# A hybrid encoder layer on one core: first norm from token-major x, first two tiles side by side, tables in the weights' buffers, residual stored from ScalarE, another end

## The chip, the cores and the metric

The kernel runs on 1 core of one Trainium2 chip. The metric is the device time of one execution in microseconds (us). A profile comes from one profiled execution, and its times count from the start of that execution's span. The engines are named as in the profile: PE is TensorE, DVE is VectorE, ACT is ScalarE, POOL is GpSimd, SP is SyncE, which only issues transfers (DMAs).

## What is computed

One layer on 512 tokens of width 2048, in float32:

```python
xn = rms_norm(x, attn_norm_g)                       # over D_MODEL = 2048
proj = xn @ w_in                                    # 2048 -> 5120
u_val, u_gate, q, k, v = split(proj)                # 1024 columns each
# group A: GLU -> depthwise conv, width 31 -> LayerNorm -> silu
y_conv = silu(layer_norm(conv31(u_val * sigmoid(u_gate))))
# group B: 2-D neighbourhood attention, 16 heads of 64, on an 8 x 64 grid,
# window 8 x 16, learned bias rpb per head
y_na = softmax(q k^T / 8 + bias) v
x = x + concat(rms_norm(y_conv), rms_norm(y_na)) @ w_out
up = conv3(rms_norm(x, ffn_norm_g) @ w_up)          # 2048 -> 2 x 5632
gate, val = split(up)
x = x + (silu(gate) * val) @ w_down                 # 5632 -> 2048
return rms_norm(x, final_norm_g)
```

## The kernel before

Activations lie with channels on the 128 partitions and the 512 tokens in the free dimension. Every float32 product is made from two parts: an operand is split into `hi`, rounded to the format of the fast matmul by ScalarE (L115 for weights, L256 for x), and `lo`, the remainder, by VectorE (L116, L257). `mm3` then issues three matmuls (hi by hi, L128; hi by lo, L131; lo by hi, L132) of 512 columns.

Weights come in units of 128 x 1024 (512 KB), one SP load each into the ring `raw` (tag "raw", NR = 9 buffers of 4 KB a partition, L92 to L117), and are split into `whi` and `wlo` (NW = 4 buffers each). A list `plan` holds the making of each unit in the order of use, and `weights()` makes them AHEAD = 3 units before they are used. All other activations of 2 KB a partition share one pool of NT = 75 tiles, `t2`. A scheduler puts the instructions of each engine in order, by priority (the place in the program, moved by `shifted`), by readiness and by free buffers; instructions under `pin` keep their order. Each engine, and each engine's own queue of DMA issues, then runs in the order written.

The stages, in order of time:

- **Head** (L248 to L287). SP loads the parameters `prm` (all per-channel factors, 336 KB), then 16 tiles of x (256 KB each) and, among them, the four units of the first two tiles of the projection, gate and value. Each x tile is multiplied by the norm's factor g1 and split. The norm's root is applied to the products later, by `rstd`.
- **Norm** (`stats1`, `rsqrt_steps`). The squares of the 16 tiles are summed on VectorE (L202), summed over partitions by matmuls with `ones` (L216), and the root is spread over the partitions by a matmul of `ones` with a diagonal `dg` (L229, L232).
- **Projections** (`project`, `glu`, `qkv`), 40 tiles of 128 output channels in the order of `ORDER`, each with a PSUM buffer of the three of tag "mm". After each half of a tile `tick` moves side work on by one step: the norm, the heads' attention, group A's LayerNorm. `gated` evacuates a gate and value pair and does the convolution of width 31 on VectorE; its results `y` lie in four buffers of the ring `raw` until group A ends. `sum_ahead` forms sums of the down weights in DRAM with GpSimd's DMAs.
- **Attention** (`attend`), one pair of heads at a time. `table` loads the bias (two DMAs of 256 KB into `t2` tiles for each half), `scores` (L414) fills the one PSUM tile `sc`, VectorE adds the bias (L421), then softmax; `turn` transposes into PSUM (L441) and copies to `pt` (L445); `values` multiplies with v.
- **Output projection** (`out_half`), twice 16 tiles. In the second, `after` adds the residual, and `turned` transposes it to tokens on partitions and stores it from SP to DRAM, four 64 KB pieces a tile (L559).
- **Up product** (`up`, `hidden`), 44 tiles, by a 2 x 2 scheme with seven products instead of eight (L656, L659). The hidden tiles go to DRAM, but for the last KEEP = 4; `again` loads them back during the last tile.
- **Down product** (`product2`, L777 to L779), the same scheme, seven products; `operand` makes the activations' split of each (L738, L739) as a part of the plan.
- **End** (`taken`, `ready`, `write`). The last product's last four steps of the sum over hidden channels are done one output block at a time; `ready` adds the residual (L829), squares (L831) and multiplies by the final norm's factor (L832), `write` forms the root (L839 to L846), scales (L851, L853) and stores, from SP and from GpSimd (L855).

## Time and profile before

| | |
|---|---|
| median of 3 runs | 2020.2 us (2019.28 to 2020.69) |
| the profiled execution: its time | 2021.06 us |
| its span | 2019.1 us |
| mean granted TensorE clock | 0.996 |
| first matmul starts | 8.04 us |
| busy: PE, DVE, ACT, POOL | 99%, 80%, 55%, 11% |
| DMA, mean | 221 GB/s |

A row of the timeline has the start, the duration, the engine and line, the operation, output <- input, how many, and in brackets the idle time before it and what ended it. A row of the waits has who waited for whom, us in total, times, and the longest. Rows of windows have the stretch, its length, then the busy time and count of PE, weight loads, DVE, ACT and POOL, the granted clock, the DMA engines' busy share and GB/s. SPq and POOLq stand for an engine's queue of DMA issues.

### The profile page before, as it was taken

To read this page: it belongs to the slowest core of one execution; us is meant where nothing else is said; L and a number is where in the kernel's file an instruction comes from. 1 tells how busy PE (TensorE), PEld (TensorE's weight loads), DVE (VectorE), ACT (ScalarE), POOL (GpSimd) and SP (SyncE) were. 2 spreads that over 40 slices of the span, in tenths; PEclk is the share of its full clock that TensorE was granted. 3 is DMA by queue.
4 is the path that set the end of the run, shared out by engine and by line. 5 is a ranking of instruction groups with operands and counts; after the bars stand their busy time and mean duration, and the time that the engine had idled before them with its cause. 6 is when DMAs were issued, how large, how long until landed. Compare 5 with 4: busy or idle time off the path is not lost.

```text
span 2019.1 us, 28450 instructions
## 1 busy us (share of the span) xinstructions
PE 1990.3 (99%) x10511; PEld 1682.7 (83%) x10511; DVE 1608.5 (80%) x2311; ACT 1104.1 (55%) x1724; POOL 230.2 (11%) x318
## 2 busy tenths in 40 slices
PE   8999999998999999999999999999999999999997
PEld 6888888877788888888888888888888888888886
DVE  7985798497556888888888888888888898886764
ACT  6244424446535666666666666666666654554663
POOL 0111111111001111111111111111110400000000
PEclk9999999999999999999999999999999999999999
DMA  7677677676758879899999898998986976665562
GB/s 257 167 222 182 171 176 207 175 191 196 232 140 214 209 204 253 248 247 256 249 255 258 245 267 233 264 242 256 259 236 192 344 261 217 213 217 192 194 212 101
DMA packets 141755, 446.81 MB, mean 221 GB/s; under 512 B 15920, under 2 KB 24112, under 8 KB 140208
## 3 DMA queue, kind: packets, MB, share of 16 engines
q1 hardware_dynamic: 98352, 293.99, 42.6%
q0 software_dynamic: 43264, 151.01, 34.4%
q8 instruction: 82, 1.34, 0.3%
q14 instruction: 57, 0.47, 0.1%
HBM read 426.07 MB, written 111.15 MB: 266 GB/s over the span
## 4 chain that ended last, share of the span: by engine, by line
PE 97%; ACT 1%; DMA 1%; DVE 1%; issue 0%; SPq 0%; POOLq 0%; POOL 0%; DVEq 0%
PE pu L656 25%; PE pu L659 12%; PE pj L128 7%; PE pj L132 7%; PE pd L778 7%; PE pd L779 7%; PE pd L777 7%; PE pj L131 7%; PE po L128 3%; PE po L131 3%; PE po L132 3%; PE pu L128 2%; PE pu L131 2%; PE pu L132 2%; PE po L454 1%; PE sc L414 1%
## 5 line engine op out<-in xcount | busy, mean ns | idle before, releaser
L115 ACT ACTIVATE whi<-raw 128x1024 fp32r<-128x1024 f32 x574 | 607.2, 1059 | 719.2 <-PE pj L131 220.6
L116 DVE TENSOR_TENSOR wlo<-raw,whi 128x1024 fp32r<-128x1024 f32 x574 | 701.1, 1222 | 295.5 <-ACT whi L115 268.2
L656 PE MATMUL pu<-xc,whi 128*128 128x512 f32 x2112 | 748.8, 399 | 0.0
L659 PE MATMUL pu<-xc,wlo 128*128 128x256 f32 x2112 | 593.2, 281 | 0.0
L656 PEld LDWEIGHTS pu<-xc,whi 128*128 128x128 f32 x2112 | 397.0, 188 | 97.0 <-issue 0.2
L659 PEld LDWEIGHTS pu<-xc,wlo 128*128 128x128 f32 x2112 | 399.1, 189 | 0.3 <-issue 0.2
L128 PE MATMUL pj<-xh,whi 128*128 128x512 f32 x640 | 254.4, 399 | 8.0 <-ACT whi L115 8.0
L131 PE MATMUL pj<-xl,whi 128*128 128x512 f32 x640 | 251.4, 393 | 0.0
L132 PE MATMUL pj<-xh,wlo 128*128 128x512 f32 x640 | 251.2, 393 | 0.0
L777 PE MATMUL pd<-whi,ho 128*128 128x512 f32 x616 | 239.5, 389 | 1.6 <-ACT ho L738 1.6
L779 PE MATMUL pd<-whi,ho 128*128 128x512 f32 x616 | 239.6, 389 | 0.6 <-DVE ho L739 0.6
L778 PE MATMUL pd<-wlo,ho 128*128 128x512 f32 x616 | 239.8, 389 | 0.0
L328 DVE SCALAR_TENSOR_TENSOR y<-ch,prm,y 128x507 f32<-128x507 f32 (+14 forms) x240 | 169.8, 739 | 3.3
L128 PEld LDWEIGHTS pj<-xh,whi 128*128 128x128 f32 x640 | 121.3, 189 | 36.3 <-ACT whi L115 9.4
L132 PEld LDWEIGHTS pj<-xh,wlo 128*128 128x128 f32 x640 | 120.9, 189 | 27.9 <-DVE wlo L116 1.5
L131 PEld LDWEIGHTS pj<-xl,whi 128*128 128x128 f32 x640 | 121.2, 189 | 24.7 <-issue 0.7
L184 POOL DMA_DIRECT2D ws<-in_w_down x88 | 79.4, 903 | 545.4 <-DMA ws<-ws 273.6
L777 PEld LDWEIGHTS pd<-whi,ho 128*128 128x128 f32 x616 | 115.7, 188 | 26.3 <-ACT ho L738 1.9
L779 PEld LDWEIGHTS pd<-whi,ho 128*128 128x128 f32 x616 | 115.7, 188 | 25.0 <-DVE ho L739 1.2
L778 PEld LDWEIGHTS pd<-wlo,ho 128*128 128x128 f32 x616 | 115.7, 188 | 24.1 <-DVE wlo L116 0.3
L605 POOL DMA_DIRECT2D raw<-in_w_up x88 | 85.3, 969 | 368.0 <-DMA raw<-in_w_up 142.2
L128 PE MATMUL pu<-xc,whi 128*128 128x256 f32 x352 | 99.7, 283 | 0.5 <-ACT xc L546 0.5
(170 smaller groups left out, 2500.4 us busy)
## 6 DMA issues: line engine op xcount, KB each, us to landing
raw<-in_w_up SPq DMA_DIRECT2D x220, 512.0 KB, 7.3
ws<-in_w_down POOLq DMA_DIRECT2D x132, 512.0 KB, 7.4
raw<-in_w_up POOLq DMA_DIRECT2D x88, 512.0 KB, 9.4
raw<-ws SPq DMA_DIRECT2D x88, 512.0 KB, 3.4
raw<-in_w_in SPq DMA_DIRECT2D x80, 512.0 KB, 5.0
raw<-in_w_down SPq DMA_DIRECT2D x66, 512.0 KB, 3.7
ws<-ws POOLq DMA_DIRECT2D x44, 512.0 KB, 7.2
raw<-in_w_out SPq DMA_DIRECT2D x32, 512.0 KB, 5.2
```

What stands on the lines that cost most here:

```text
L115: i = nc.scalar.activation(hi[:, :n], raw[:, :n], AF.Copy)
L116: j = nc.vector.tensor_sub(lo[:, :n], raw[:, :n], hi[:, :n].bitcast(F32))
L128: i = nc.tensor.matmul(ps, hi[:, a], mh, start=start, stop=False, skip_group_check=more)
L131: nc.tensor.matmul(ps, hi[:, a], ml, start=False, stop=False, skip_group_check=more)
L132: return nc.tensor.matmul(ps, lo[:, a], mh, start=False, stop=stop, skip_group_check=more)
L328: nc.vector.scalar_tensor_tensor(y[:, a:b], h[:, a + j - PAD:b + j - PAD], prm[:, o + j:o + j + 1], y[:, a:b], op0=ALU.mult, op1=ALU.add)
L605: nc.gpsimd.dma_start(a[c], w_up[f, q2], accum_op=ALU.add)
L656: i = nc.tensor.matmul(ps, hi[:, w], m, start=k == 0 and not more, stop=False, skip_group_check=more)
L659: i = nc.tensor.matmul(ps[:, :H], lo[:, w], m[:, :H], start=False, stop=k == U - 1, skip_group_check=more)
L777: nc.tensor.matmul(ps[i], h[:, t], wh[:, d], start=start and not more, stop=False, skip_group_check=more)
L778: nc.tensor.matmul(ps[i], h[:, t], wl[:, d], start=False, stop=False, skip_group_check=more)
L779: return nc.tensor.matmul(ps[i], h[:, tl], wh[:, d], start=False, stop=stop, skip_group_check=more)
```

## The change

Five things are changed together.

- **Head.** ScalarE does a one-element copy behind the memset of `ones`, and TensorE 11 matmuls of 128 x 128 on `ones` into an unused PSUM tile. The norm's factor `g1` is loaded by itself from ScalarE's queue, the rest of `prm` after x. The gate and the value tile run side by side (`first_glu`): at each tile of x six matmuls, three for each. The first half of their weights is loaded in pieces of 2, 2 and 4 tiles of 128 columns.
- **First norm.** `stats1` loads x a second time, with tokens on partitions (`xn`, eight loads of 512 KB into the ring `raw`), squares on ScalarE with the sum along the free dimension, and forms the root from there (`root_steps`).
- **Tables.** The two tables of a half come in one load of 512 KB into one buffer of the ring `raw`. The copy of the transposed softmax to `pt` gets an earlier priority.
- **Residual and hidden tiles.** The residual is one DRAM tensor, stored with one DMA a tile from ScalarE's queue. `again` loads six hidden tiles at a time instead of eight, and the down product's first operand is made during the second product of the last up tile.
- **End.** `ready` in the last product comes at an earlier priority; for one block of each pair the factor g is applied in `write` together with the scale. The root is taken from the sum directly, with scale and bias on ScalarE, and one product is fused. Stores go out from SP and ScalarE.

```diff
+WARM = 11
+SOONER = 100
...
-    nc.sync.dma_start(prm, par)
+    g1 = consts.tile([P, KD], F32, name="g1")
+    nc.scalar.dma_start(g1, par[:, :KD])
...
     nc.vector.memset(ones, 1.0)
+    idle = t2("idle")
+    nc.scalar.activation(idle[:, :1], ones[:, :1], AF.Copy)
+    ps = psm.tile([P, S], F32, tag="mm", name="warm")
+    for _ in range(WARM):
+        nc.tensor.matmul(ps[:, :P], ones, ones, start=True, stop=True)
...
+    def split_x(k):
         x1.append(t2("x"))
-        last = pin(nc.sync.dma_start(x1[k], xT[k]))
+        i = pin(nc.sync.dma_start(x1[k], xT[k]))
...
+    def piece(n, k0, k1):
+        m = (k1 - k0) * P
+        raw, hi, lo = t2("we")[:, :m], t2("weh", F32R)[:, :m], t2("wel", F32R)[:, :m]
+        pin(nc.sync.dma_start(raw, w_in[n, :, k0 * P:k1 * P]))
+        pin(nc.scalar.activation(hi, raw, AF.Copy))
+        pin(nc.vector.tensor_sub(lo, raw, hi.bitcast(F32)))
+        return [(hi, lo, k - k0) for k in range(k0, k1)]
...
+    for ks, ws in (((0,), (0, 2)), ((1,), (2, 4)), ((2, 3), (4, 8)), (range(4, 8), ())):
+        for k in ks:
+            split_x(k)
+        for j, n in enumerate((NC_, 0)):
+            if ws:
+                early[j] += piece(n, *ws)
+    for j, n in enumerate((NC_, 0)):
+        raw, i = raw_unit(w_in[n, :, U * P:2 * U * P], U * P)
...
+    for k in range(U, KD):
+        last = split_x(k)
+    last = pin(nc.sync.dma_start(prm, par))
...
     def stats1():
-        for k in range(KD):
-            sum_sq(acc1, x1[k], k == 0)
-        for _ in range(3):
-            yield
-        rstd.append((yield from rsqrt_steps(acc1, D, "rstd1")))
+        part = sm.tile([P, S // P, 2], F32, tag="ss", name="ss")
+        for t in range(S // P):
+            for i in range(2):
+                x = t4([P, D // 2], "xn")
+                nc.sync.dma_start(x, xn[t * P:(t + 1) * P, i * D // 2:(i + 1) * D // 2])
+                nc.scalar.activation(x, x, AF.Square, accum_out=part[:, t, i:i + 1])
+            if t < S // P - 1:
+                yield
+        sums = sm.tile([P, S // P], F32, tag="s1", name="s1")
+        nc.vector.tensor_reduce(sums, part, axis=AX.X, op=ALU.add)
+        rstd.append((yield from root_steps(sums, D, "rstd1")))
...
+    def first_glu():
+        two = [psm.tile([P, S], F32, tag="mm", name="pj") for _ in range(2)]
+        for u in range(KD // U):
+            ws = weights(), weights()
+            for k in range(U):
+                kk = u * U + k
+                for ps, w in zip(two, ws):
+                    hi, lo, at = w[k]
+                    m = mm3(ps, (hi, lo), at, xs[kk][0], xs[kk][1], kk == 0, kk == KD - 1)
+            for _ in range(2):
+                tick(m)
+        late.append(lambda: gated(0, *two))
...
-                nc.scalar.activation(pt, ps, AF.Copy)
+                with shifted(-SOONER):
+                    nc.scalar.activation(pt, ps, AF.Copy)
...
         def table(b0):
-            for j in range(2):
-                tb = t2("tab").rearrange("p (i k) -> p i k", i=2)
-                i = nc.sync.dma_start(tb, tab[2 * p + j][:, b0 // 2:b0 // 2 + 2])
-                if p == 0:
-                    pin(i)
-                tabs.append(tb)
+            tb = t4([P, 2, 2, 2 * P], "tab")
+            i = nc.sync.dma_start(tb, tab[2 * p:2 * p + 2, :, b0 // 2:b0 // 2 + 2].rearrange("h p k c -> p h k c"))
+            if p == 0:
+                pin(i)
+            tabs.append(tb)
...
-        o = d % (S // P) * P
-        for t in range(S // P):
-            nc.sync.dma_start(xt[t][d * P // S][:, o:o + P], r[:, t, :])
+        nc.scalar.dma_start(xt[:, :, d * P:(d + 1) * P].rearrange("t p k -> p t k"), r)
...
-            plan.append(lambda c=c, k=k: (unit2(c, k), operand(c, k)))
+            plan.append(lambda c=c, k=k: (unit2(c, k), pre.pop(0) if pre else operand(c, k)))
...
+    pre = []
+
     def again(at, i):
-        for _ in range(8):
+        if at == 1:
+            pre.extend(operand(TURN2[0], k) for k in order2[:KEEP // 2 - 1])
+        for _ in range(6):
...
-            nc.vector.tensor_mul(x[i], x[i], gs[d])
+            if i not in fused:
+                nc.vector.tensor_mul(x[i], x[i], gs[d])
             yield
...
         nc.vector.tensor_reduce(v, sq[th][:, t], axis=AX.X, op=ALU.add)
+        nc.scalar.activation(r, v, AF.Sqrt, scale=1.0 / D, bias=eps)
         nc.vector.tensor_scalar(v, v, 1.0 / D, EPS, op0=ALU.mult, op1=ALU.add)
-        nc.scalar.activation(r, v, AF.Sqrt)
         nc.vector.reciprocal(r, r)
-        nc.vector.tensor_mul(y, v, r)
-        nc.vector.tensor_mul(y, y, r)
+        nc.vector.scalar_tensor_tensor(y, v, r, r, op0=ALU.mult, op1=ALU.mult)
         nc.vector.tensor_scalar(y, y, -0.5, 1.5, op0=ALU.mult, op1=ALU.add)
         nc.vector.tensor_mul(y, y, r)
-        for d in range(Q):
+        for d in reversed(range(Q)):
             for dh in range(2):
-                x = ys[dh][t * Q + d]
+                i = t * Q + d
+                x = ys[dh][i]
                 if dh:
+                    nc.scalar.activation(x, x, AF.Copy, scale=y)
+                elif i in fused:
+                    nc.vector.scalar_tensor_tensor(x, x, y, gs[d], op0=ALU.mult, op1=ALU.mult)
+                else:
                     nc.vector.tensor_scalar(x, x, y, None, op0=ALU.mult)
-                else:
-                    nc.scalar.activation(x, x, AF.Copy, scale=y)
                 o = (Q * dh + d) * S
-                queues[dh].dma_start(out[(2 * th + t) * P:(2 * th + t + 1) * P, o:o + S], x)
+                (nc.scalar if dh else nc.sync).dma_start(out[(2 * th + t) * P:(2 * th + t + 1) * P, o:o + S], x)
...
+    fused = [i for i in range(2 * Q) if i % Q == Q - 1]
     for i in product2(5, a, False):
-        for _ in ready(e3, a, 0, 0, (i,)):
-            pass
+        with shifted(-100):
+            for _ in ready(e3, a, 0, 0, (i,), fused):
+                pass
```

79 lines of the change are left out of this document (35 added, 44 removed).

## The prediction

> **What bounds the kernel now.** I read the page first, then TensorE's waits, then the timeline at each place where TensorE stood still.
>
> ```profile
> span 2019.1 us, 28450 instructions
> PE 1990.3 (99%) x10511; PEld 1682.7 (83%) x10511; DVE 1608.5 (80%) x2311; ACT 1104.1 (55%) x1724; POOL 230.2 (11%) x318
> ...
> PE pj L128 <- ACT whi L115: 8.0, 1, 8.0
> PE sc L414 <- DVE s L421: 5.1, 1, 5.1
> PE pd L777 <- ACT ho L738: 1.6, 1, 1.6
> PE trv L402 <- ACT pt L445: 1.4, 1, 1.4
> PE pd L779 <- DVE ho L739: 0.6, 1, 0.6
> ```
>
> TensorE (PE) is busy for 99% of the span, so only what it waits for, and matmuls that run slowly, can be saved; VectorE (80%) and ScalarE (55%) matter where they hold it up. Not busy are 28.8 us (2019.1 - 1990.3): 8.0 before the first matmul, 8.7 in the four other waits, and 12.1 that lie almost all after the last matmul. Busy time hides one more loss, a slow clock after each long idle. The change removes almost no matmul, so all of it must be found in these places. The sum is made on the profiled execution (span 2019.1, its own time 2021.06); I carry the difference over to the median, 2020.2.
>
> **The start.**
>
> ```profile
> 0.84 0.17 DVE L104 MEMSET ones<- 128x128 f32 x1 [0.84 <-PEq L947]
> ...
> 4.59 1.28 ACT L256 ACT_TABLE_LOAD   x1 [4.59 <-DMA x<-in_xT]
> 5.88 0.72 ACT L256 ACTIVATE xh<-x,prm 128x512 fp32r<-128x512 f32 x1
> ...
> 6.93 1.06 ACT L115 ACTIVATE whi<-raw 128x1024 fp32r<-128x1024 f32 x1 [0.32 <-DMA raw<-in_w_in]
> ...
> 8.04 0.80 PE L128 MATMUL pj<-xh,whi 128*128 128x512 f32 x1 [8.04 <-ACT whi L115]
> ...
> 15.40 0.39 PE L128 MATMUL pj<-xh,whi 128*128 128x512 f32 x1
> ...
> prm<-in_par SPq DMA_DIRECT2D x1, 336.0 KB, 3.2
> ...
> 508.34 0.43 PE pj L128
> ...
> 36.25 0.23 PE pj L128
> 42.14 0.86 PE st L232 x2
> ```
>
> The last three rows are steps of the chain of waits: a 512-column matmul holds TensorE for 0.43 us while its clock is down and for 0.23 after. From 8.04 to some time before 15.40, the first of the matmuls that last 0.39, it was down: about 6.5 us at half rate lose 3.3. With 8.04 that makes 11.3 us lost at the head.
>
> After the change ScalarE loads its table at about 1 us (a one-element copy behind the memset of `ones`), not at 4.59. The 336 KB of parameters leave the head of SP's queue; x0 stands there, and `g1` (8 KB) goes through ScalarE's. The parameters took 3.2 us from issue to landing, so x0 (256 KB, issued at about 0.7) lands at about 3.7. Then xh (0.72) and a 256-column piece of weights (0.41, as L738 below) allow a first product at about 5. The 11 matmuls on `ones` stand ahead of it: 512 fp32 columns took 0.86 us at full clock, so 128 take 0.22, 0.43 at half, and 11 take 4.7: from 1.1 to 5.8. The first real matmul comes at 5.8 rather than 8.04. The clock took some 6.5 us of work to come up here and 5 after 504 (below), so it is up between 6.1 and 7.6; real work is then slow for 0.3 to 1.8 us, half of it lost; I take 0.6. Loss 6.4 instead of 11.3: a gain of 4.9. I take off 0.5 for the splits: each x tile now feeds 6 matmuls (1.4 us), ScalarE needs 0.72 + 2 x 1.06 / 8 = 1.0 per tile, 1.2 with the small pieces, so only the first are tight. **+4.4** (3 to 5.5).
>
> The Trainium skill, "TensorE: Matmul & The Clock Gate", Part 1, says that the clock is halved until one free-running window of about 3.4 us has been busy. By that it opens 3.4 to 6.8 us after the first warm-up matmul, at 4.5 to 7.9; at its earliest the warm-up itself would end at about 5.2, the term be an estimated 5.6 and the time 1.2 us less. The two ramps of this trace, 5 and 6.5 us, lie in its upper half, and the sum goes by them.
>
> **The first norm.**
>
> ```profile
> 38.06 0.79 PE st L216 x8
> ...
> 43.67 0.69 DVE L313 TENSOR_TENSOR gate<-pj,rstd 128x512 f32<-128x512 f32 x1 [2.40 <-ACT rstd L236]
> ...
> 16.00:18.00 2.00, 2.00 (x11) 1.65 (x10) 2.00 (x4) 2.00 (x5) 0.00 (x0) 1.00 1.04 385
> 20.00:40.00 20.00, 20.00 (x93) 16.36 (x92) 18.54 (x29) 15.36 (x24) 0.00 (x0) 1.00 0.73 277
> ```
>
> The eight L216 steps leave TensorE: **+0.8**. VectorE loses 15 additions that nobody waited for: 0. ScalarE squares 8 x 1024 columns (about 1.06 + 0.19 each, 10 us) where it squared 16 x 512: 0. New are 8 loads of 512 KB, 4.2 MB on SP's queue between the weights and in the weights' 9 buffers. There is room (the last column of the windows: 277 GB/s moved from 20 to 40 us, 385 while x came), but the last lands late: x, early weights and parameters, 6.6 MB, end at about 21 us; 8 loads and 3 units of weights add 11 x 1.3, so 35.4. The square (1.25) and then sum, root, the diagonal, its matmul and the gate's product (5.5 us from L216's end to L313's end) give 42. The fourth tile can start only when that product has freed one of three PSUM buffers, and with the head shortened it wants to at 6.4 + 0.5 + 144 x 0.23 = 40. Part of the 5.5 was the wait for a turn on TensorE, so **-1.5** (0 to -4).
>
> **The tables.**
>
> ```profile
> 471.37 17.59 SPq L110 DMA_DIRECT2D raw<-in_w_out  x5
> 489.01 1.10 SPq L464 DMA_DIRECT2D tab<-in_tab  x2
> ...
> 501.10 0.69 DVE L421 SCALAR_TENSOR_TENSOR s<-sc,tab 128x512 f32<-128x512 f32 x1 [5.96 <-DMA tab<-in_tab]
> ...
> 504.26 2.08 PE L414 MATMUL sc<-k,q 64*128 64x256 f32 x8 [5.14 <-DVE s L421]
> ...
> 504.00:506.00 2.00, 1.74 (x8) 1.27 (x8) 1.47 (x5) 1.77 (x9) 0.00 (x0) 0.50 1.11 292
> 506.00:510.00 4.00, 4.00 (x14) 2.93 (x13) 2.82 (x5) 2.33 (x5) 0.00 (x0) 0.59 0.75 206
> ...
> SPq L110 <- DVE wlo L116: 50.8, 7, 14.5
> ...
> SPq L464 <- PE pj L132: 0.6, 2, 0.3
> ...
> DMA to landing us min/median/max: 4.5/5.8/12.1
> ```
>
> Head pair 6's first tables were issued at 489.0 and landed at 501 (12.1 us, the longest of all tables; the median is 5.8). VectorE stood 6.0 us on them, TensorE 5.1. The granted clock (the third column from the right in the windows) is 0.50 and 0.59 until 510: 5 us at half rate, 2.5 more. Together 7.6. Why so late? SP's queue waits, its rows with SPq, say two things: it stood up to 14.5 us behind weights whose buffer VectorE had not freed, and the table itself waited for a matmul L132 of a projection, the last reader of an xh. So the shared 2 KB tiles were all taken, and the table got its place only as the last projection gave up x. In the weights' ring it needs no such tile and can go among the five loads of 471 to 489; issued by 488 it lands by 494 at the median, and TensorE wants the result at 499 (504.26 - 5.14). I take the whole stall less 0.6 for a load twice as large: **+7.0** (0 to 7.6; the lower end if the queue still holds it up). The price on the other side is under the rivals.
>
> `pt` copied sooner: at 530 the copy stood behind a weight split, **+1.4** (0 to 1.6; the listed wait).
>
> **The residual from ScalarE.** 64 issues leave SP; 16 enter ScalarE's queue, where each holds the weight split behind it for the length of an issue. SP's issues above took 0.5 (1.10 for two), so 8 us over 16 tiles of output, on an engine that is idle for 45% of the span, with weights split ahead: 0 (-1 to +0.5).
>
> **The switch to the down product.**
>
> ```profile
> 1585.98 1.06 ACT L115 ACTIVATE whi<-raw 128x1024 fp32r<-128x1024 f32 x1 [1.49 <-PE pu L656]
> ...
> 1587.20 0.41 ACT L738 ACTIVATE ho<-uy 128x256 fp32r<-128x256 f32 x1
> ...
> 1587.66 0.51 PE L777 MATMUL pd<-whi,ho 128*128 128x512 f32 x1 [1.61 <-ACT ho L738]
> ...
> 1589.93 0.42 DVE L739 TENSOR_TENSOR ho<-uy,ho 128x256 fp32r<-128x256 f32 x1
> ```
>
> The first operand is split only as it is wanted; the change makes it products earlier. That ends the gap from 1585.9 to 1587.66 and the wait of 0.6 behind it, 2.4. Late next is the second operand: ready at 1590.35, or some 0.4 earlier without the first in front, while TensorE, begun at 1585.9, wants it after 12 + 2 matmuls of 0.23, at 1589.1: 0.8 comes back. **+1.6** (1 to 2.6).
>
> **The other end.**
>
> ```profile
> 2008.14 0.69 DVE L829 TENSOR_TENSOR xr<-xr,pd 128x512 f32<-128x512 f32 x1
> ...
> 2010.91 0.15 DVE L839 TENSOR_REDUCE rsv<-sq 128x1 f32<-128x4 f32 x1
> ...
> 2012.49 0.88 DVE L851 TENSOR_SCALAR xr<-xr,rsy 128x512 f32<-128x512 f32 x2
> ...
> 2013.38 1.16 POOL L855 DMA_DIRECT2D out_T<-xr  x2 [1.82 <-DVE xr L851]
> ```
>
> After the last sum (2008.83) and its square (0.8) the reduction could start at 2009.6; it starts at 2010.91 because other rows' scales and the product by g (L832) stand ahead. Fused and moved, they don't. The chain to the scale, 1.6 us here, loses a scalar step and a product of 0.2: scale at 2010.8 instead of 2012.5. The four last stores then go out through SP and ScalarE, the second of ScalarE behind its first issue and second scale (0.7 each as xh, 0.4 an issue), at about 12.6, against 14.0 on POOL. **+1.9** (0.5 to 2.5; the low end if only the chain is shorter).
>
> **Sum.** 4.4 + 0.8 - 1.5 + 7.0 + 1.4 + 1.6 + 1.9 = 15.6 us. 2020.2 - 15.6 = **2004.6 us**.
>
> **The rivals.** *The table stall stays*: what held SP was a burst on ScalarE and VectorE around 472 to 485, which the change leaves. For it: the wait of 14.5. Against: the table waited for a tile too. The 7.0 go: 2011.6. *The head gives back its gain*: the norm's loads come behind the weights, and TensorE stops at the fourth tile for 4 us and more, then runs at half clock for some 5: 4 + 2.5 instead of 1.5, 2009.6. *Slower*: the tables starve the weights.
>
> ```profile
> raw<-in_w_in SPq DMA_DIRECT2D x80, 512.0 KB, 5.0
> ```
>
> Of the ring's 9 buffers the convolution holds 4 until about 490, tables up to 2, so 3 are left. Weights land 5.0 us after issue and are used at 5.5 us each (24 matmuls), so three give 16.5 us of cover; it decides where a burst holds the splits longer than some 11 us, as that wait of 14.5 did. Each such stop would cost about what the one at 498 cost, 7.6; three over 16 tables, 22.8 against 15.6 gained, give 2027.4. *It does not do what it says*: the order on the queues hardly moves, and only the warm-up and the end count: 2020.2 - 4.4 - 1.9 = 2013.9.
>
> A second rule speaks against one detail: "DMA: Bandwidth & Descriptors", Specifications, in the Trainium skill, names 512 bytes as the least transfer for full rate, and `g1` has 64 per partition; no run shown here has such a load. If it is 1 us late, the warm-up still covers it.
>
> **How the numbers follow.** As forecast 0.55, table stall 0.2, head 0.1, little done 0.07, slower 0.08. The forecast's own range, from the terms' bounds, is 2000 to 2010. To hold 8 in 10 it goes up to the table rival and past it: 1999.5 to 2012.5. 0.2% is 4 us, about what a measurement can tell from no change; under 2016.2 lie all cases but the last and parts of the others' tails: faster 0.87, same 0.06, slower 0.07.
>
> **What would show it.** Right: first product at about 5.8, matmuls at 0.23 spacing by 8; no wait of L414's line on VectorE of over 1 us near 500 and no granted clock of 0.5 there; no wait on L738's line; last store's issue some 4.5 us after the last matmul. Wrong: a wait of TensorE near 40 us on the gate's product, waits on whi or wlo between 100 and 490, or a tail as long as before.

## The result, and the profile after

The median went from 2020.4 to 2015.35 us (15 runs of each: 2018.82 to 2025.21, and 2014.21 to 2020.34). The ratio is 0.9976, with a 95% interval of 0.9968 to 0.9984. The change is faster, but by 5 us and not by the 15.6 of the forecast, and 2015.35 lies above its range (1999.5 to 2012.5). The profiled execution has a span of 2014.3 (2019.1 before) and a time of its own of 2016.07 (2021.06).

First the span and the busy times, from the page of the profile after:

```profile
span 2014.3 us, 28373 instructions
...
PE 1994.4 (99%) x10525; PEld 1685.5 (84%) x10525; DVE 1599.6 (79%) x2296; ACT 1105.2 (55%) x1729; POOL 226.1 (11%) x310
```

Then TensorE's waits after (us in total, times, longest):

```profile
PE pd L821 <- DVE ho L777: 4.0, 2, 2.6
PE pj L138 <- DVE gate L352: 1.4, 1, 1.4
PE warm L112 <- DVE eps L114: 1.1, 1, 1.1
PE pj L142 <- DVE wlo L126: 0.8, 1, 0.8
PE st L237 <- DVE dg L234: 0.6, 1, 0.6
...
PE pd L819 <- ACT ho L776: 0.5, 1, 0.5
```

The waits of 8.0 (first weights), 5.1 (scores on the table), 1.4 (`pt`) and 1.6 (`ho` on L738) are gone. In their place stand waits that were not there: 1.4 and 0.6 at the fourth tile, 0.8 on a weight's remainder, and 4.0 on `ho` at the start of the down product. All its waits add up to 10.4 us now against 17.7 before, which is 7.3 less, and the span is only 4.8 shorter. The clock is not the difference: work of the layer ran at half clock for 7.8 us now against 11.2 before. But TensorE's busy time grew by 4.1 (1990.3 to 1994.4), above all by the warm-up: its 11 matmuls fill the 4.7 us from 1.06 to 5.78, count as busy and do no work of the layer. Where time was won and lost is therefore read by setting the start of the same matmul in both traces side by side:

| The same matmul | Before | After | After minus before |
|---|---|---|---|
| first of the projection | 8.04 | 5.78 | -2.26 |
| 21st of the projection | 15.85 | 11.75 | -4.10 |
| first of the third tile | 33.08 | 30.52 | -2.56 |
| in the middle of the third tile | 39.71 | 35.96 | -3.75 |
| in the middle of the fourth tile | 51.50 | 51.78 | +0.28 |
| at 107 us | 106.10 | 107.34 | +1.24 |
| last of the projection | 509.25 | 504.49 | -4.76 |
| output projection, 72 matmuls in | 534.08 | 526.99 | -7.09 |
| last of the up product | 1585.78 | 1578.28 | -7.50 |
| down product, 96 matmuls in | 1610.48 | 1607.44 | -3.03 |
| last of all | 2007.72 | 2004.74 | -2.97 |
| end of the span | 2019.1 | 2014.3 | -4.8 |

Two things went as forecast: the 8.3 us between 107 and 534, and the 1.8 at the end. The gain of the head was lost again, 4.0 at the fourth tile and 1.0 at 101 us, and 4.5 more were lost at the switch to the down product.

**The head.** It was 4.1 us ahead at the 21st matmul and only 2.56 when the first two tiles were done. The loads seem to have set the pace there. ScalarE and TensorE after, in one timeline, then the window from 12 to 14 us:

```profile
11.62 0.63 ACT L265 ACTIVATE weh<-we 128x512 fp32r<-128x512 f32 x1 [0.53 <-DMA we<-in_w_in]
12.29 2.76 ACT L256 ACTIVATE xh<-x,g 128x512 fp32r<-128x512 f32 x4
...
13.07 0.50 PE L138 MATMUL pj<-xh,weh 128*128 128x512 f32 x1 [0.24 <-ACT xh L256]
```

```profile
12.00:14.00 2.00, 1.47 (x6) 0.69 (x5) 1.65 (x3) 1.96 (x4) 0.00 (x0) 1.00 1.04 416
```

ScalarE waited for a piece of weights, the fifth tile of x landed only at 12.27, and TensorE waited for its split; the transfers ran at 391 to 416 GB/s from 12 to 23 us. That the loads are the cause is read off this trace; no run tests it. Of the 3.75 in the third tile, 0.9 are the eight matmuls of L216, which the kernel before has there and the change has not.

**The fourth tile.** TensorE after, each row with start, duration and, in brackets, the idle time before and what ended it:

```profile
5.78 0.77 PE L138 MATMUL pj<-xh,weh 128*128 128x512 f32 x1
...
7.33 0.39 PE L141 MATMUL pj<-xl,weh 128*128 128x512 f32 x1
...
41.17 0.39 PE L142 MATMUL pj<-xh,wlo 128*128 128x512 f32 x1
42.19 1.13 PE L237 MATMUL st<-dg,ones 128*128 128x512 f32 x2 [0.63 <-DVE dg L234]
44.73 0.79 PE L138 MATMUL pj<-xh,whi 128*128 128x512 f32 x1 [1.41 <-DVE gate L352]
```

The start is the one forecast: first product at 5.78, spacing 0.23 soon after 7. The third tile ends at 41.4. Then TensorE stands for the diagonal, and again for the gate's product that frees a PSUM buffer. The granted clock falls to half behind it (third column from the right in the windows; TensorE's busy time is the third number):

```profile
42.00:44.00 2.00, 1.13 (x2) 0.30 (x2) 1.29 (x3) 0.63 (x2) 0.00 (x0) 1.00 1.02 406
44.00:48.00 4.00, 3.27 (x8) 2.60 (x9) 2.72 (x5) 1.91 (x3) 0.00 (x0) 0.57 0.82 325
```

What TensorE waits for is the end of a chain on ScalarE and VectorE: last square, table load, root, gate (after):

```profile
37.48 1.06 ACT L306 ACTIVATE xn<-xn 128x1024 f32<-128x1024 f32 x1
...
38.65 1.28 ACT L225 ACT_TABLE_LOAD   x1
...
43.35 0.60 ACT L239 ACTIVATE rstd<-st 128x512 f32<-128x512 f32 x1 [2.25 <-PE st L237]
```

```profile
43.98 0.69 DVE L352 TENSOR_TENSOR gate<-pj,rstd 128x512 f32<-128x512 f32 x1 [0.71 <-ACT rstd L239]
```

The gate's product starts at 43.98. Before, it started at 43.67, with TensorE 3.75 us less far. The new norm was not ready sooner than the old one had been; the head only brought TensorE to it sooner.

**The tables.** After: the issue of the table that had been late (the first of head pair 6), then VectorE's addition that had waited for it, then the time from issue to landing of all sixteen tables:

```profile
449.53 0.38 SPq L504 DMA_DIRECT2D tab<-in_tab  x1
...
493.56 0.68 DVE L212 TENSOR_TENSOR acc<-acc,sq 128x512 f32<-128x512 f32 x1
494.16 0.68 DVE L461 SCALAR_TENSOR_TENSOR s<-sc,tab 128x512 f32<-128x512 f32 x1
```

```profile
DMA to landing us min/median/max: 3.4/4.9/9.7
```

The table is issued at 449.5, where before it was issued at 489.0, and landed at 455.3. The addition that had waited 5.96 for it follows another one with no wait. The longest landing, 9.7 instead of 12.1, belongs to a later table, for which nobody waited. TensorE's clock is 1.00 from 498 to 506.

**The switch to the down product.** Before, VectorE waited for `g3` as well, but with three splits of `ho` just ahead of the wait, and TensorE did not stop:

```profile
1595.59 0.42 DVE L739 TENSOR_TENSOR ho<-h,ho 128x256 fp32r<-128x256 f32 x1
...
1596.59 0.42 DVE L739 TENSOR_TENSOR ho<-h,ho 128x256 fp32r<-128x256 f32 x1
...
1598.66 0.42 DVE L739 TENSOR_TENSOR ho<-h,ho 128x256 fp32r<-128x256 f32 x1
1602.55 0.43 DVE L812 TENSOR_SCALAR g<-g 128x512 f32<-128x512 f32 x1 [3.47 <-DMA g<-in_g]
```

After, VectorE and TensorE in one timeline:

```profile
1597.70 0.39 PE L820 MATMUL pd<-wlo,ho 128*128 128x512 f32 x1
...
1599.90 0.43 DVE L855 TENSOR_SCALAR g<-g 128x512 f32<-128x512 f32 x1 [5.87 <-DMA g<-in_g]
1600.25 0.42 DVE L777 TENSOR_TENSOR ho<-h,ho 128x256 fp32r<-128x256 f32 x1
...
1600.72 0.58 PE L821 MATMUL pd<-whi,ho 128*128 128x512 f32 x1 [2.63 <-DVE ho L777]
```

VectorE stood from 1594.0 on for a load that only the very end needs (the final norm's factor, tensor `g3`, of which two tiles get their sign changed), the next split of `ho` stood behind it, and TensorE ran dry at 1597.9. From 1601 to 1605 the granted clock averages 0.57.

**The end.** After, the last row sum's way to the last stores (VectorE, ScalarE and its queue, one timeline):

```profile
2007.09 0.16 DVE L881 TENSOR_REDUCE rsv<-sq 128x1 f32<-128x4 f32 x1 [0.79 <-ACT sq L874]
...
2008.50 1.33 ACT L893 ACTIVATE xr<-xr,rsy 128x512 f32<-128x512 f32 x2 [0.93 <-DVE rsy L887]
...
2009.25 0.95 ACTq L899 DMA_DIRECT2D out_T<-xr  x2
```

From the last matmul's start (2004.74) the reduction comes at 2.35 and the scale at 3.76; before they came at 3.19 (2010.91 - 2007.72) and 4.77 (2012.49).

### The profile page after: what moved, and what is told of

Read it like the earlier page. It is cut to its first block, busy times and chain, and to the rows that moved or that the text cites. A ratio compares the mean times of both kernels' runs of the same rounds, so it can differ in the third digit from the quotient of the medians.

```text
span 2014.3 us, 28373 instructions
## 1 busy us (share of the span) xinstructions
PE 1994.4 (99%) x10525; PEld 1685.5 (84%) x10525; DVE 1599.6 (79%) x2296; ACT 1105.2 (55%) x1729; POOL 226.1 (11%) x310
## 4 chain that ended last, share of the span: by engine, by line
PE 94%; DMA 2%; DVE 2%; ACT 1%; issue 0%; SPq 0%; DVEq 0%; ACTq 0%
PE pu L694 25%; PE pu L697 12%; PE pd L821 7%; PE pd L819 7%; PE pd L820 7%; PE pj L138 6%; PE pj L141 6%; PE pj L142 6%; PE po L138 3%; PE po L141 3%; PE po L142 3%; PE pu L141 2%; PE pu L138 2%; PE pu L142 2%; DVE y L367 1%; DMA xn<-in_xn 1%
## 5 line engine op out<-in xcount | busy, mean ns | idle before, releaser
L138 PE MATMUL pj<-xh,whi 128*128 128x512 f32 x624 | 246.8, 398 | 1.4 <-DVE gate L352 1.4
L142 PE MATMUL pj<-xh,wlo 128*128 128x512 f32 x624 | 243.7, 390 | 0.8 <-DVE wlo L126 0.8
L141 PE MATMUL pj<-xl,whi 128*128 128x512 f32 x624 | 244.4, 392 | 0.1
L821 PEld LDWEIGHTS pd<-whi,ho 128*128 128x128 f32 x616 | 116.0, 188 | 29.3 <-DVE ho L777 5.3
```

The lines of the kernel that those rows point to most:

```text
L138: i = nc.tensor.matmul(ps, hi[:, a], mh, start=start, stop=False, skip_group_check=more)
L141: nc.tensor.matmul(ps, hi[:, a], ml, start=False, stop=False, skip_group_check=more)
L142: return nc.tensor.matmul(ps, lo[:, a], mh, start=False, stop=stop, skip_group_check=more)
L821: return nc.tensor.matmul(ps[i], h[:, tl], wh[:, d], start=False, stop=stop, skip_group_check=more)
```

## The experiments

My theory after the result: the two losses are waits of one engine that works strictly in order, on something that is not urgent (VectorE on g3) or not ready (the norm's root), and the clock that falls behind the stop. The main rival: VectorE is simply short of time in both places, so that whatever is moved, it stops TensorE somewhere else. Medians below stand beside the runs of the kernel before on the same chip, which were 2019.92, 2020.62, 2019.44 and 2019.57 in the four groups.

### The switch

**The sign change later** (`late_sign`): g3's tiles are loaded as in the change, and their sign is changed eight steps later.

```diff
             nc.sync.dma_start(g, g3[:, d * S:(d + 1) * S])
-            if d >= Q:
-                nc.vector.tensor_scalar(g, g, -1.0, None, op0=ALU.mult)
             gs.append(g)
             yield
+        for _ in range(8):
+            yield
+        for g in gs[Q:]:
+            nc.vector.tensor_scalar(g, g, -1.0, None, op0=ALU.mult)
+            yield
```

> The changed kernel, with the sign change of the two loaded tiles of g3 moved eight steps later in the program, its loads left where they are. My account: VectorE runs in order and stood 5.9 us at the sign change, waiting for the load of g3, with the split of the next operand behind it; TensorE then idled 2.6 us at 1597.7 us and ran about 3.4 us at half clock. With the sign change later, that idle and the slow clock go and the time falls by 4 to 5 us to about 2011. Rival: the split of the operand itself waited for its hidden tile, which comes later since six instead of eight are loaded at a time; then TensorE waits for the same split all the same and the time stays within 1.5 us.

Measured: 2010.79 (ratio 0.9957, 0.9942 to 0.9972), span 2009.3, 5.0 under the change. TensorE's wait there:

```profile
PE pd L821 <- DVE ho L777: 1.4, 1, 1.4
```

The wait of 2.6 is gone and the clock stays up there. One moved instruction is worth as much as the whole change. At the switch the rival falls with it: nothing else stops TensorE there for longer than before (24.65 us from the last up product to 96 matmuls into the down product, against 24.70 in the kernel before).

**The switch undone, and half undone** (`old_switch`, `eight`).

```diff
-        if at == 1:
-            pre.extend(operand(TURN2[0], k) for k in order2[:KEEP // 2 - 1])
-        for _ in range(6):
+        for _ in range(8):
```

In `eight` only the 6 becomes 8, and the two lines stay.

> The change with the switch to the down product as in the kernel before: no operand made ahead, and eight, not six, earlier steps' operands taken back at each step. My account (six a step leave fewer splits of ho ahead of the sign change of g3, on whose load VectorE stands): the splits stand ahead of the sign change again, the stop of 2.8 us at 1597.7 and the half clock behind it go, the first operand is late again by some 2.2 as in the kernel before, and the span is 2014.3 - 4.5 = 2009.8 (2009 to 2011). Rival (the stop comes from the stores and loads round it, not from six for eight): the stop stays and the span is 2014 or more.

> The change with eight for six alone, the first operand still made ahead. VectorE's order then has more splits of ho ahead of the sign change, each worth some 2.7 us of matmuls, so the stop at 1597.7 is gone and what is left of the switch is the wait of 1.4 and 0.5 that the late-sign run also had: span 2009.3 (2008.5 to 2010.5). If the stop at 1597.7 stays, six for eight is not its cause, and making the first operand ahead is.

Measured: `old_switch` 2011.15 (0.9966, 0.9946 to 0.9985), span 2008.9, of which 4.5 were won between the last up product and the 96th matmul behind it. VectorE's wait for g3, from the view of that line:

```profile
DMA g<-in_g: 3.2, 1
```

It is there still, from about 1590.7 to 1593.9, and costs nothing, as in the kernel before: enough splits stand ahead of it. `eight`: 2011.95 (0.9949, 0.9932 to 0.9966), 8 runs from 2009.69 to 2017.87. Its profiled run, with a span of 2016.1, was one with another stop (at 700 us, below), and its clock fell at 1588 for 3.4 us; the stop at 1597.7 is gone in it. So six for eight put the wait in the way. In both runs the gaps at the first operands come to 2.6 us (1.8 and 0.8 with no operand made ahead; 0.7 and 1.9 with one): making the first one ahead only moved the wait behind it. The profile puts the 1.9 down to VectorE's `vl` (L708), not to a split of `ho`; what makes it late was not tested.

**Both operands ahead** (`late_two`): the late sign, and `order2[:KEEP // 2]` for `order2[:KEEP // 2 - 1]`.

> The change with the sign change of g3 eight steps later (as in the run before) and both first operands of the down product, not one, made ahead. In the run with the late sign the switch still had a wait of 1.4 on ho (L777) and one of 0.5 on L776. My account (the second operand is late because it is split only when wanted): the 1.4 goes and the span is 2009.3 - 1.4 = 2007.9 (2007.5 to 2008.4). Rival (the two engines have no time to spare there; what is made earlier makes a weight split later): the wait moves to a weight or to the last up products and the span is 2009.0 to 2010.

Measured: 2009.7 (0.9952, 0.9937 to 0.9967), the lowest median of all kernels here. Three of its four spans were 2006.8, 2007.4 and 2008.4. The profiled one was 2011.9, with a stop of 3.2 and half clock at 700. Between the last up product and the end of the down product it gains 5.7 on the change, where `late_sign` gained 4.5; so the second operand is worth 1.2. A wait of 1.3 stays behind the two operands:

```profile
PE pd L819 <- DVE vl L708: 1.3, 1, 1.3
```

### The fourth tile

**The old norm in the new head, and all loads first** (`old_norm`, `norm_first`). The one squares the sixteen tiles and adds them on VectorE, as before, with no second load of x. The other issues the eight loads of `xn` before any square:

```diff
+        got = {}
+        for t in range(S // P):
+            for i in range(2):
+                x = got[t, i] = t4([P, D // 2], "xn")
+                nc.sync.dma_start(x, xn[t * P:(t + 1) * P, i * D // 2:(i + 1) * D // 2])
         for t in range(S // P):
             for i in range(2):
-                x = t4([P, D // 2], "xn")
-                nc.sync.dma_start(x, xn[t * P:(t + 1) * P, i * D // 2:(i + 1) * D // 2])
+                x = got[t, i]
```

> The changed kernel with the first norm's sum formed as before (16 squares of 512 columns, added up by VectorE, eight small matmuls) and no second load of x. My account: the second load of x, 4.2 MB that lands by 37.4 us, is what makes the root late; without it TensorE's waits at 42 to 45 us (0.6 and 1.4 us and the half clock after them) go and the time falls by 3 to 4 us. Rival: the fourth tile now comes 3.7 us earlier and any way of forming the root is too late for it; then TensorE waits as long or longer at that place and the time is within 1.5 us of the changed kernel or above it.

> The changed kernel with the eight loads of the norm ahead of two units of weights on the queue instead of four before and four behind. Both accounts of the stall at the fourth tile say that the last load lands 2.6 us earlier, at about 34.8 us, and the gate's product ends at about 42. My account: TensorE then waits less than 0.7 us there and its clock stays up; the third tile's second unit of weights lands at about 36 and costs about 1 us instead; the time falls by 2 to 4 us. Rival: the weights that now come behind the loads cost as much as the stall did, and the time stays within 1 us.

Measured: 2018.9 (0.9994, 0.9983 to 1.0006) and 2017.37 (0.9993, 0.9984 to 1.0002), both slower than the change where my account had them 2 to 4 faster. With the old norm the diagonal comes later still:

```profile
PE st L237 <- DVE dg L234: 1.5, 1, 1.5
PE pj L138 <- DVE gate L347: 1.4, 1, 1.4
```

VectorE's additions end at 40.5 there, mixed with weight splits; the gate's product starts at 46.93, 3 us after the change's. With all loads first the stop is another one, on a weight's `hi` part:

```profile
PE pj L138 <- ACT whi L125: 2.7, 1, 2.7
```

The weights landed behind the second load of x, 4.2 MB, and ScalarE took the splits up only after all squares and the table load, at 38.05. My account of "late loads" was too simple: the transfers run without a gap, one 512 KB load landing every 1.28 us (410 GB/s) until about 48, and whichever is put first, the other is late.

**A fourth bank** (`fourth_bank`): the fourth tile is summed in a PSUM bank that only attention uses later.

```diff
-        ps = psm.tile([P, S], F32, tag="mm", name="pj")
+        ps = psa.tile([P, S], F32, tag="po", name="pj") if n == 1 else psm.tile([P, S], F32, tag="mm", name="pj")
```

> The change with one thing altered: the fourth tile (value columns of the second pair) is summed in the PSUM bank that attention uses later (tag po), so that it need not wait until the gate's product has emptied one of three banks. My account (the root is ready only at about 43.4, and with the shortened head TensorE wants a bank at 41.2): the wait of 1.4 on the gate (L352) goes, TensorE idles for less than 1 us between 40 and 50, the granted clock stays at 1.0 there, the loss of 4.1 us in that stretch shrinks to under 0.7, and the span is 2010.5 to 2011.3 (3 to 3.8 less than the change's 2014.3). Rival (the eight loads of x keep the weights late, so TensorE runs into a missing weight split next, as in the run with all loads first): a wait on whi between 42 and 55 takes its place and the span stays above 2013.

Measured: 2022.46 (1.0007, 0.9997 to 1.0017), span 2019.6; the worst of all. The wait at 41 is gone, the fourth tile starts at 41.74, and two others take its place, at 54 and 103:

```profile
PE pj L142 <- DVE wlo L126: 7.1, 2, 3.8
```

Both are VectorE's. With a bank free, the scheduler put the diagonal's matmul 18 matmuls later; the gate's product then started at 47.51, and gates and convolutions of the first two pairs stood in a burst ahead of the weights' remainders. So the rival holds in part: from 44 to 110 VectorE has next to no reserve (in the change it is busy for 62.6 of these 66 us), and a later root brings the stops back elsewhere.

**Half of the norm's loads** (`half_norm`). The kernel leaves out half of each row, so its norm is that of half of x.

```diff
-            for i in range(2):
+            for i in range(1):
...
-        nc.vector.tensor_reduce(sums, part, axis=AX.X, op=ALU.add)
-        rstd.append((yield from root_steps(sums, D, "rstd1")))
+        nc.vector.tensor_reduce(sums, part[:, :, 0:1], axis=AX.X, op=ALU.add)
+        rstd.append((yield from root_steps(sums, D // 2, "rstd1")))
```

> The change with half of the first norm's loads and squares (four of 512 KB, the first 1024 columns of each row; the norm is then that of half of x). The order on every engine is otherwise the change's. In the change each of the last loads landed 1.28 after the one before it; four fewer should bring the last one in at 32.3 instead of 37.4 and the diagonal (L234) by 38 instead of 42.2. The matmul of the diagonal (L237) still stands behind the whole third tile in TensorE's order, at about 41.2, so its copy (0.60) and the gate's product (0.69) still come after it: the fourth tile starts at about 43.1 instead of 44.73. If lateness of the loads is all that the stop is made of, it is gone (the fourth tile at 41.4, span 2014.3 - 4.1 = 2010.2). If the place of L237 holds the rest, as I now think, TensorE idles some 1.5 us, the clock may stay up, and the span is 2011.6 to 2013.3. Rival of the run with the fourth bank (VectorE lacks time between 45 and 110 whatever the root does): wlo waits near 54 and 101 grow and the span stays above 2013.5.

Measured: 2013.67 (0.9967, 0.9955 to 0.9979), span 2010.2 in the profile. The fourth tile starts at 43.21, as expected with the place of L237 as the cause, and the clock stays up:

```profile
42.00:44.00 2.00, 0.79 (x3) 0.67 (x4) 0.69 (x1) 1.97 (x3) 0.00 (x0) 1.00 0.12 49
44.00:48.00 4.00, 4.00 (x19) 3.27 (x18) 3.52 (x6) 1.92 (x4) 0.00 (x0) 1.00 0.00 0
```

Four loads less won 2.96 at the fourth tile, half of it by the clock. VectorE's row for the diagonal:

```profile
36.48 0.87 DVE L234 TENSOR_SCALAR dg<-ident,rsy 128x128 f32<-128x128 f32 x4
```

The wait of 1.4 on the gate remains though the diagonal is ready at 37.35: the matmul of the diagonal stands behind the whole third tile in TensorE's order. The rest of the span's gain (1.2) came at the switch, where the same stop did not lower the clock this time.

**No warm-up** (`no_warm`): WARM = 0.

> The change without the 11 matmuls on ones. If the clock rises after some microseconds of work, whoever's work it is: first real product at about 5.0, clock up only at 10 to 11.5 instead of 6.97, so some 1.5 us less has been done when it is up; the fourth tile then comes later and waits less, and the span is within 1 us of the change's 2014.3. Rival (the clock rises at a fixed time after the start, and the warm-up does nothing): clock up at about 7 all the same, and the first tiles earlier by 0.8.

Measured: one run, 2019.72, span 2018.0, with the stop at 700 in it. The first product came at 4.98, full clock at 10.89 instead of 6.97, and the fourth tile started at 44.57 (44.73 with the warm-up). At the end of the projection both stand at 504.5. So in this one run the warm-up raises the clock sooner, and the wait for the norm takes all that it gains.

**The old head** (`old_head`): all of the change but the first 45 us.

> The change with the first 45 us of the kernel before: its order of loads, its first tiles one after the other, its norm from x with features on partitions, no warm-up. All the rest is the change's. At 107 us the change stood 1.24 behind the kernel before, so the head and the norm together cost 1.24: the span is 2014.3 - 1.2 = 2013.1 (2012.3 to 2013.9). If the head is worth anything, it is above 2014.3; if the head's gain as forecast (3 to 5) were only hidden by something later, 2016 to 2018.

Measured: 2016.35 (0.9984, 0.9972 to 0.9996), span 2015.4, from 2012.8 to 2019.7 over ten runs. Not the 2013.1 that I expected, and not to be told from the change's 0.9976 either. Its profiled run had a stop of its own at 32 on VectorE:

```profile
PE pj L135 <- DVE wlo L119: 1.9, 1, 1.9
```

Head and norm together are therefore worth about nothing, within 1.5 us either way; the 1.24 that I read from two profiles is not confirmed. The other traces say the same: the 401st matmul of the projection, behind all that head and norm can do, starts between 104.2 and 106.4 in the five profiles with the old head (`before`, `tables_only`, `old_head`, `best3`, `best3_sp`) and between 104.3 and 106.2 in five with the new (`after`, `late_sign`, `late_two`, `old_switch`, `eight`). A difference of 1 or 2 us there, between two single profiles, says nothing.

### The tables, and the versions put together

**The tables alone** (`tables_only`): the kernel before, with each pair's two tables in one tile of the weights' ring.

```diff
-            for j in range(2):
-                tb = t2("tab").rearrange("p (i k) -> p i k", i=2)
-                i = nc.sync.dma_start(tb, tab[2 * p + j][:, b0 // 2:b0 // 2 + 2])
+            tb = t4([P, 2, 2, 2 * P], "tab")
+            i = nc.sync.dma_start(tb, tab[2 * p:2 * p + 2, :, b0 // 2:b0 // 2 + 2].rearrange("h p k c -> p h k c"))
```

> The kernel before, with the tables in the weights' buffers and nothing else of the change. My account: the stall of TensorE at 498.7 us (5.1 us idle and about 2.5 us at half clock) ends, so the span falls by 6 to 8 us and L414 has no wait of over 1 us. Rival: the queue of loads, not the place for the table, held it; then the stall stays or moves and the time is within 2 us of before. Second rival: the tables starve the weights; then TensorE waits on whi or wlo between 60 and 490 us appear and the time is 3 us or more above before.

Measured: 2014.04 (0.9971, 0.996 to 0.9982), span 2011.0, 8.1 off. This part alone does as much as the whole change. From the 401st matmul of the projection to 72 matmuls into the output projection it takes 421.46 us, exactly as the change does; the kernel before takes 429.79. The wait on `pt` at 530 went with it, with no earlier copy; so the 1.4 put down to that copy belongs to the tables.

**All three repairs** (`best2`): late sign, both operands, fourth bank.

> All three together: late sign, both operands ahead, fourth tile in a bank of its own. If the three places are independent of each other, the parts add: 2014.3 - 5.0 - 1.4 - 3.5 = 2004.4 of span (2003.5 to 2005.5), which is the time the forecast gave. If shortening the first stretch only moves a stop to a later one (the stop at 101 us grows), 2006 to 2008.

Measured: 2016.61 (0.999, 0.998 to 0.9999), span 2014.7: the stops at 54 and 103 are here too, 7.1 together, and take what the switch gives.

**Before's first 45 us with the rest repaired** (`best3`, `best3_sp`): the second stores the residual from SP as before.

```diff
-        nc.scalar.dma_start(xt[:, :, d * P:(d + 1) * P].rearrange("t p k -> p t k"), r)
+        for t in range(S // P):
+            nc.sync.dma_start(xt[t, :, d * P:(d + 1) * P], r[:, t, :])
```

> Before's first 45 us, the tables, the earlier pt copy, the residual from ScalarE and the tail of the change, with the sign change of g3 late and both operands of the down product ahead. From the run with both operands (undisturbed near 700: spans of 2006.8 to 2008.4) less the 1.24 of the head: 2006.3 (2005.5 to 2007.2). If the head of the change helps after all, 2008 to 2010.

> The same with the residual stored from SP in four pieces of 64 KB for each tile, as before, instead of from ScalarE in one. The forecast put this part at 0 (-1 to +0.5): within 0.5 of the run above. Rival: the stop of 1.5 to 3.3 us that TensorE has at 700 in some executions (ScalarE waits for a tile whose store from ScalarE took 10.7 us to land) belongs to the store from ScalarE; then it does not show here in any run, and the spread of the runs is below 2 us, while the run above has some that are 4 us slower.

Measured: 2010.39 (0.995, 0.9935 to 0.9965), span 2008.6, and 2011.14 (0.9954, 0.9935 to 0.9972), span 2008.5. They tie with each other and with `late_two`; all three beat both kernels, the change by some 3 to 6 us and the kernel before by 8 to 11. The 2006.3 expected of the first was too low by the 1.24 of the head, which is not there, and by about 1 more.

**The stop at 700.** Four of the profiled runs have it (`norm_first`, `late_two`, `no_warm`, `eight`), and it may be behind some slow single runs that were not traced. ScalarE and TensorE in `late_two`:

```profile
699.52 0.42 ACT L586 ACTIVATE xc<-b 128x256 fp32r<-128x256 f32 x1 [3.45 <-DMA xt<-xt]
```

```profile
702.89 1.08 PE L594 MATMUL trx<-ident,x 128*128 128x128 f32 x4 [3.16 <-DVE x L603]
```

ScalarE needs the tile of a residual store that took 10.7 us to land (6.3 is the median of these stores). All four such profiles (1.5 to 3.2 us) are among the thirteen with the store from ScalarE and none among the three with it from SP. But `best3_sp` had one run at 2017.81, which was not traced, so whether the store from SP is free of it stays open.

## Why the prediction was wrong, step by step

- **The start, +4.4 (3 to 5.5): mechanism right, size too high.** First product at 5.78 against 5.8, clock up near 7. But only 2.6 us were left at the end of the first two tiles and 2.85 just ahead of L216. The term that was too small is the 0.5 "for the splits": 1.5 were lost from 12 to 22 us, where splits waited for loads, which the step did not price. What was left was then counted as if nothing behind it were waiting to be late.
- **The first norm, -1.5 (0 to -4): failed.** The forecast knew when the last load lands (35.4 forecast, 37.4 found; each of 512 KB takes 1.28 us and they run without a gap from 3 on) and when TensorE arrives (40 forecast, 41.2 found), and put the gate's product's end at 42 (44.7 found). A wait near 40 us on the gate's product was the prediction's own first sign of being wrong. The error has three parts: the loads' 2 us, the order of L237 behind the third tile, and the half clock behind the stop. `half_norm` parts them: with the loads out of the way the stop of 1.4 stays, by the order, and the clock holds. Together with the 1.0 at 101 us, where VectorE's convolutions held a weight's remainder for 0.8, the step took 5.0, all that the start and L216 had gained. This was the rival "the head gives back its gain", which was held at 0.1 and priced at 6.5 in place of 1.5, at 2009.6; with the switch as forecast the time would have been near it. That the old chain reached the gate's product only at 43.67, with TensorE some 4 us later than now, stood in the prediction's own row, and it should have set the price: up to the time at which that product is ready, an earlier TensorE only waits longer.
- **L216 off TensorE, +0.8: right.** 0.9 found in the third tile, and lost with the start's gain.
- **The tables and `pt`, +7.0 and +1.4: the sum right, one reason wrong.** 8.3 found between 107 and 534; `tables_only` shows that all of it is the tables'. The account of the tables held, and by more than forecast: issued at 449.5, not just "by 488". That the 1.4 came in too was luck, since the earlier copy had no part in it. The rival "the tables starve the weights" did not come true: on SP's queue loads of weights stood 12.4 us, eleven times, for a table's buffer, but TensorE had no wait on `whi` or `wlo` of over 1 us between 100 and 490.
- **The residual, 0 (-1 to +0.5): right.** From 72 matmuls into the output projection to the first up product the change takes 175.17 us against 175.33 before, and `best3` 175.01 against 175.45 in `best3_sp`: 0.2 to 0.4 won. Another 0.25 comes in evenly over the up product, also in `best3_sp`, so it is not this store's. In single runs there is a stop of 3 us at 700 that may belong to it.
- **The switch, +1.6 (1 to 2.6): failed, with the wrong sign.** -4.5. The step looked at ScalarE and the first two operands alone. It left out the second half of the edit, six for eight, and the queue that this shifts: VectorE's, in which the sign change of `g3` waits for a transfer that takes 10.3 us to land in the median. A wait that was there before, and harmless, was put in TensorE's way. `late_sign` (5.0 back), `old_switch` and `eight` show it from three sides. Also the first operand's gain was too high: it only moved the wait behind it (2.6 in all, with and without), and only both together gain 1.2.
- **The end, +1.9: right.** 1.8 found; the reduction comes 0.84 sooner after the last matmul, the scale 1.01.

The sum in this pair of profiles: -1.2 for head and norm, 8.3, 0.4 from the output projection to the last up product, -4.5, 1.8 make the 4.8 of the span. Head with norm (3.7 forecast) and the switch make up 4.9 and 6.1, together just over the 10.8 by which the forecast was off.

The range was too narrow by its own terms: with each term at its lower bound the gain is 0.3 us, not the 10 at which "2000 to 2010" ends, and 2015.35 lies well inside the terms.

## What to carry to other kernels

Before an earlier start is counted as a gain, ask what the first consumer behind it waits for, and take the time at which that was ready in the old trace: up to that point the gain is not yours. When operands are reordered or their number per step is changed, read the whole order of each in-order engine around them and look for an instruction that waits on a transfer; it costs nothing while enough work stands ahead of it, and everything behind it once there is less. A repair that frees a resource (a bank, an earlier load) also moves what a scheduler places by it, so the stop has to be looked for again.

## What the runs showed of the hardware

TensorE's clock fell behind stops in which TensorE was never idle for long. In the change's stop at 41 the longest idle time was 1.41 us, and the clock was down for the next 3.4. The same stop, by the windows from 40 to 50 us of `eight` and of `old_switch` (TensorE busy, then as above the clock third from the right):

```profile
40.00:50.00 10.00, 7.21 (x23) 4.86 (x22) 6.82 (x17) 5.63 (x8) 0.00 (x0) 0.83 0.74 287
```

```profile
40.00:50.00 10.00, 7.18 (x29) 4.97 (x29) 6.77 (x17) 5.62 (x8) 0.00 (x0) 1.00 0.75 295
```

The idle time is equal (two gaps of 1.4 in each), and in the second the clock stayed at full speed, so that 29 matmuls and not 23 fell into the window. Each fall lasts 3.4 us or twice that. The stop at the switch shows the price: from the last up product to 96 matmuls into the down product `late_sign`, without the stop, takes 24.7 us; `half_norm`, `norm_first` and `fourth_bank`, with the stop and no fall, 27.7 to 28.0; `after`, `old_norm`, `no_warm` and `old_head`, with both, 29.0 to 29.3. A stop and a fall there cost 4.4 and a stop alone 3.2, and four of seven profiles had the fall:

```profile
1597.54 0.50 PE L821 MATMUL pd<-whi,ho 128*128 128x512 f32 x1 [2.59 <-DVE ho L777]
...
1598.00:1602.00 4.00, 3.92 (x17) 2.80 (x16) 3.21 (x5) 1.06 (x1) 1.39 (x3) 1.00 1.03 395
```

These two rows are of `half_norm`: a stop as long as the change's, and a clock of 1.00 behind it. The Trainium skill, "TensorE: Matmul & The Clock Gate", Part 1, gives 3.4 us as a window that runs free of the program, and one idle window as the condition for the slow clock. The length and the chance agree with these runs; an idle window of 3.4 us was not needed here. On the way up: with the same warm-up, begun at 1.06, the first record of full clock lay between 4.2 and 7.0 us in the runs of this study, a spread of 2.8; the soonest is 3.1 behind the first of these matmuls, 0.3 less than a whole window.

The 8 KB of `g1`, 64 bytes a partition, took as long as a large load (KB each and median time from issue to landing, after):

```profile
g<-in_par ACTq DMA_DIRECT2D x1, 8.0 KB, 3.0
```

That is 0.2 us later than x0, 256 KB issued at the same time; the warm-up covered it, and the first product came when forecast.
